# Sixteen copies out of PSUM move from VectorE to ScalarE in the attention, S5 and convolution parts of a decoder layer

## The chip, the cores and the metric

The kernel runs on one core of one Trainium2 chip. The metric is the device time of one execution in microseconds (us); the figure for a kernel is the median of several runs. PE is the matrix engine (TensorE), DVE is VectorE, ACT is ScalarE, POOL is GpSimd, and SP is the engine that issues most of the transfers.

## The reference

One layer of a hybrid decoder trunk with 512 tokens and a model width of 1024, all in float32. What is computed is a token mixer with three causal branches on the same normalised input, then a gated feed-forward part:

```python
h = rms_norm(x, pre1_w[l]) * (1.0 + sc1) + sh1
z = h @ w_in                       # one projection feeds all three branches
gq, gk, gv, ga, gr, mq, mk, mv, mi, mf, mo, su, zg = _split(z, IN_SIZES)
g_log = log_sigmoid(ga @ gla_a2 + gla_a_b) / GLA_GATE_NORM
o_gla = gla_attention(gq, gk, gv, g_log)           # chunked linear attention with decay
qk = silu(causal_dwconv(concat([mq, mk]), ml_conv_w, ml_conv_b))   # four taps
h_ml = mlstm_memory(qk_q, qk_k, mv, mi + ml_i_b, mf + ml_f_b)
y_s5 = gelu(s5_ssm(su, ...)); y_s5 = y_s5 * sigmoid(y_s5 @ s5_glu_w + s5_glu_b)
merged = gates0 * (y_gla @ proj_gla) + gates1 * (y_ml @ proj_ml) + gates2 * (y_s5 @ proj_s5)
x = x + (1.0 + gt1) * rms_norm(merged @ w_out, post1_w[l])
... swiglu feed-forward in the same sandwich of norms
```

The chunked gated attention needs the queries `gq`, the keys `gk` and the cumulated decay `cum`; the S5 branch needs its input `su`, and for each of four blocks of groups an impulse response, a matrix of transitions and a matrix of states.

## The kernel before

**Products.** Every float32 product is made of three matmuls of split operands: `passes` writes hi*hi, hi*lo and lo*hi into one bank of PSUM (lines 422 to 424, and 454 to 456 where the tokens are the stationary side). A weight arrives by a transfer as `raw`; ACT writes its upper part `hi`, and DVE the difference `lo`, L220, `lo<-raw,hi`. A product with `lo` therefore waits for a transfer, for ACT and for DVE. A bank of PSUM (`mm_bank` for the big products, `ax_bank` for auxiliary ones) is free again when its last reader is done.

**Stages.** The head (to about 66 us) normalises x and runs the "sweep": one pass over the input channels that fills six banks at once, `sweep_ps[0:2]` with gq, `[2:4]` with gk, `[4]` with the small gate inputs (ga, ii, lf), `[5]` with the first part of su. Then comes the gated attention (to about 190 us): the copies qT and kT, the decay (`log_sig`, whose first step is `t<-ax,pv` on ACT, L935 being its small product on PE), seven levels of pairwise scores (L1106, L1111), the running states `Sg` from kdT and gv (L1153, L1177), the normed output `og`, and its transposes (L1200). The S5 branch follows (to about 296 us) in five steps: `states(step-1)`, `params(step)`, `outputs(step-1)`. `states` makes PE's state product (L1283), then on DVE the rotated x5 and y5, a scan `v`, and the shifted `Xs`. `params` makes on DVE CA and `wp` out of four outer products o0 to o3, then a small `bs`, on PE the impulse responses (L1254), on some engine the copy `ks` of them, and a transfer of ks to memory and back as the matrix M. The mLSTM branch with the convolutions, the output projection and the feed-forward part come last.

**Order.** Between these steps the code calls `fill(n)`, which takes the next jobs from a list: gate products (`z` jobs, `ev_gate`), branch projections (`p` jobs, `merged`), the remaining inputs (`ev_gv`, `ev_gr`, `ev_su`, `ev_conv`) and, through DVE's `gacc`, the modulation rows. The order written so is not the order run: outside the regions fixed by hand, the framework's scheduler places the instructions of each engine by its own estimate of when they are ready. So an instruction that moves to another engine shifts others that the diff doesn't name. What is in the same order before and after: everything up to about 66 us, and everything behind about 344 us.

**Helpers.** `cp` (L232) is a copy on DVE, `ts` (L223), `tt` (L220) and `stt` (L226) are its operations with one scalar, two tensors, and both; `af` (L229) is an activation on ACT. As all calls go through them, the profile names these lines, and an instruction is told by its tiles (`kdT<-ax`). `st3` holds small statistics; `rstd` turns the sums of squares (ACT's `junk<-og`) into the norm's factors.

Of the kernel before, what the change touches and what calls it, by code (L numbers as in the profile page):

```python
# [8 lines left out]
AF = mybir.ActivationFunctionType  # L9
OP = mybir.AluOpType  # L10
# [166 lines left out]
def _body(tc, A, out):  # L177
    nc = tc.nc
    act, dve, pool, pe, sp = nc.scalar, nc.vector, nc.gpsimd, nc.tensor, nc.sync
    from contextlib import ExitStack  # L180
    with ExitStack() as ctx:
        _emit(tc, nc, ctx, ExitStack, A, out, act, dve, pool, pe, sp)


def _emit(tc, nc, ctx, ExitStack, A, out, act, dve, pool, pe, sp):
# [23 lines left out]
    def slot(name="s", dt=F32, tag="s"):  # L209
        return pools[tag].tile([128, 512], dt, tag=tag, name=name)  # L210
# [4 lines left out]
    def ax_bank(name="ax"):  # L215
        return axp.tile([128, 512], F32, tag="ax", name=name)


    def tt(e, o, a, b, op):
        e.tensor_tensor(out=o, in0=a, in1=b, op=op)  # L220

    def ts(e, o, a, s1, s2, op0, op1=OP.bypass):
        e.tensor_scalar(out=o, in0=a, scalar1=s1, scalar2=s2, op0=op0, op1=op1)  # L223

    def stt(o, a, s, b, op0, op1):
        dve.scalar_tensor_tensor(out=o, in0=a, scalar=s, in1=b, op0=op0, op1=op1)  # L226

    def af(o, i, f, **kw):
        act.activation(out=o, in_=i, func=f, **kw)  # L229

    def cp(o, i, e=dve):
        e.tensor_copy(out=o, in_=i)  # L232
# [12 lines left out]
    def P(name, i=None, n=1, rows=slice(0, 128)):  # L245
        o, w = _PV[name]
        return pv[rows, o:o + w] if i is None else pv[rows, o + i:o + i + n]

    def C(name, rows=slice(0, 128)):
        o, w = _CS[name]  # L250
        return cs[rows, o:o + w]
# [240 lines left out]
    for j, (c0, w) in enumerate(STRIPS):  # L492
        n = 512 // w
# [66 lines left out]
    w, h, u, r = (st[:, 4 * i:4 * i + 4] for i in range(4))  # L560
# [49 lines left out]
    sweep_ps = []  # L610
# [41 lines left out]
    def ev_conv(f):  # L652
        def e(ps):
            u = slot("conv", tag="v")
            w = lambda j: P("conv_w", f * 4 + j)
            ts(dve, u, ps, w(3), P("conv_b", f), OP.mult, OP.add)
            for j in range(3):
                d = 3 - j
                stt(u[:, d:512], ps[:, 0:512 - d], w(j), u[:, d:512], OP.mult, OP.add)
            af(u, u, AF.Silu)  # L660
            conv[f] = u
        return e
# [3 lines left out]
    def ev_su(f):  # L666
        def e(ps):
            u = slot("su")
            cp(u.rearrange("p (a n) -> p a n", a=8)[:, ::-1], ps.rearrange("p (n a) -> p a n", a=8))
            sp.dma_start(out=su_d[f].rearrange("a p n -> p a n"), in_=u.rearrange("p (a n) -> p a n", a=8))  # L670
            U[f] = upool.tile([128, 512], F32, tag="U", name="U")
            sp.dma_start(out=U[f], in_=su_d[f].rearrange("a (c g) n -> (a c) (g n)", g=8))
        return e
# [241 lines left out]
    qT, kT = {}, {}  # L915
    for p in range(2):
        qT[p], kT[p] = slot("gq"), slot("gk")
        af(qT[p], sweep_ps[p], AF.Copy, scale=0.125)
        cp(kT[p], sweep_ps[2 + p])
    ts(dve, ii[0:4], ii[0:4], P("i_b", rows=slice(0, 4)), None, OP.add)  # L920
    fill(1)
    cum = {}
# [10 lines left out]
    for p in range(2):  # L933
        ps = ax_bank()
# [149 lines left out]
    qk, qE, ecum, kdT, Sg = {}, {}, {}, {}, {}  # L1084
# [30 lines left out]
    n = 0  # L1115
# [15 lines left out]
    for p in range(2):  # L1131
        cv = cum[p].rearrange("p (t i) -> p t i", t=4)
        kd = slot("kd")
        kdv = kd.rearrange("p (t i) -> p t i", t=4)
        tt(dve, kdv[:, 0:3], cv[:, 0:3, 127:128].broadcast_to([128, 3, 128]), cv[:, 0:3], OP.subtract)
        af(kd[:, 0:384], kd[:, 0:384], AF.Exp, scale=1.0 / 16)
        tt(dve, kd[:, 0:384], kd[:, 0:384], kT[p][:, 0:384], OP.mult)
        ecum[p] = slot("ecum", tag="y")
        af(ecum[p], cum[p], AF.Exp, scale=1.0 / 16)
        qE[p] = slot("qE", tag="y")  # L1140
        tt(dve, qE[p], ecum[p], qT[p], OP.mult)
        ps = ax_bank()
        for t in range(3):
            pe.transpose(out=ps[:, t * 128:(t + 1) * 128], in_=kd[:, t * 128:(t + 1) * 128], identity=ident)
        kdT[p] = slot("kdT", tag="y")
        cp(kdT[p][:, 0:384], ps[:, 0:384])
    FL.until("gv")
    fill(2)
    for p in range(2):
        Sg[p] = slot("Sg", tag="y")  # L1150
        for t in range(3):
            ps = ax_bank()
# [13 lines left out]
    for t in range(4):  # L1166
        ps = [ax_bank(), ax_bank()]

        for h in range(4 if t else 0):
            p, hh = h // 2, h % 2  # L1170
# [3 lines left out]
        for h in range(4):  # L1174
            p, hh = h // 2, h % 2
            a = (t % 2) * 2 + hh
# [36 lines left out]
    def big(name):  # L1213
        return b4p.tile([128, 1024], F32, tag="b4", name=name)
# [3 lines left out]
    def outer(dst, a_r, a_i, k0, pr, sign):  # L1218

        pb = lambda x: x[:, pr, k0:k0 + 8].unsqueeze(3).broadcast_to([128, 4, 8, 16])  # L1220
        ab = lambda x: x[:, pr].unsqueeze(2).broadcast_to([128, 4, 8, 16])
        x = [slot(f"o{i}") for i in range(4)]
        w = lambda y: y.rearrange("p (a k c) -> p a k c", a=4, k=8)
        for i, (m, n) in enumerate(((P0, a_r), (P1, a_i), (P0, a_i), (P1, a_r))):
            tt(dve, w(x[i]), pb(m), ab(n), OP.mult)
        f = lambda y, r: y[r].rearrange("p (a n) -> p a n", a=4)
        d = dst.rearrange("p (a g n) -> p a g n", g=2, n=128)
        for g, r, q in ((0, even, odd), (1, odd, even)):
            tt(dve, d[r, :, g], f(x[0], r), f(x[1], r), OP.subtract)
            if sign > 0:  # L1230
                tt(dve, d[q, :, g], f(x[2], r), f(x[3], r), OP.add)
            else:
                stt(d[q, :, g], f(x[2], r), -1.0, f(x[3], r), OP.mult, OP.subtract)
# [3 lines left out]
    def params(b):  # L1237
        pr = slice(4 * b, 4 * b + 4)
        CA[b] = big("CA")
        outer(CA[b], s5c[:, 0], s5c[:, 1], 0, pr, -1)  # L1240
        wp = big("wp")
        outer(wp, bb[:, 0], bb[:, 1], 1, pr, 1)
        bs = slot("bs")
        bv = bs[:, 0:256].rearrange("p (g c) -> p g c", c=32)
        pool.memset(bs[:, 0:256], 0.0)
        b2 = bv[:, :, 0:16].rearrange("p (a g) c -> p a g c", g=2)
        for g, r, q in ((0, even, odd), (1, odd, even)):
            cp(b2[r, :, g], bb[r, 0, pr])
            cp(b2[q, :, g], bb[r, 1, pr])
        fill(1)  # L1250
        kp = ax_bank()
        for g in range(8):
            q = (g % 4) * 32
            mm(kp[q:q + 32, (g // 4) * 128:(g // 4 + 1) * 128], lhsT=bv[:, g], rhs=CA[b][:, g * 128:(g + 1) * 128],  # L1254
               start=True, stop=True, tile_position=(0, q))
        ks = slot("ks")
        cp(ks[:, 0:256], kp[:, 0:256])
        for j in range(2):
            stt(ks[:, j * 128:j * 128 + 16], C("dmask"), P("s5_d", 2 * b + j), ks[:, j * 128:j * 128 + 16],
                OP.mult, OP.add)  # L1260
        for q in range(4):
            sp.dma_start(out=kd_d.rearrange("(j q) c x -> q c j x", q=4)[q, :, 2 * b:2 * b + 2, 128:256],
                          in_=ks[q * 32:q * 32 + 16, 0:256].rearrange("p (j x) -> p j x", j=2))
        WT[b] = big("WT")
        for h in range(2):
            ps = ax_bank()
            for g in range(4):
                o = (h * 4 + g) * 128
                pe.transpose(out=ps[:, g * 128:(g + 1) * 128], in_=wp[:, o:o + 128], identity=ident)
            (lambda o, i: af(o, i, AF.Copy))(WT[b][:, h * 512:(h + 1) * 512], ps)  # L1270
        Mt[b] = big("M")
        for a in range(8):
            sp.dma_start(out=Mt[b][a * 16:(a + 1) * 16].rearrange("p (g x) -> p g x", g=8),
                         in_=kd_d[8 * b:8 * b + 8, :, 16 + 16 * a:144 + 16 * a].rearrange("g c x -> c g x"))
        fill(2)
# [49 lines left out]
    for step in range(5):  # L1325
        if step >= 1:
            states(step - 1)
        if step < 4:
            params(step)
        if step >= 1:  # L1330
            outputs(step - 1)
# [59 lines left out]
    ps = ax_bank()  # L1391
# [7 lines left out]
    for p in range(2):  # L1399
        ps = ax_bank()  # L1400
# [15 lines left out]
    for p in range(2):  # L1416
        qw[p] = mslot("qw")
        stt(qw[p], conv[p], 0.125, wI[p], OP.mult, OP.mult)
        ps = ax_bank()
# [8 lines left out]
    for p in range(2):  # L1428
        mem[p] = mslot("mem")
        for t in range(3):  # L1430
            ps = ax_bank()
# [277 lines left out]
    n = 22  # L1709
    for k in range(n - HOLD):  # L1710
        w = S.get(ffo_i[k], 4)
# [34 lines left out]
```

## Time and profile before

| | |
|---|---|
| median of three runs | 912.28 us (910.48 to 912.75) |
| the profiled execution | 910.4 us, of which 908.6 us are the span and 1.8 us lie around it |
| PE busy | 888.7 us, 98% of the span |
| DVE busy | 575.7 us, 63% |
| ACT busy | 331.0 us, 36% |
| mean granted TensorE clock | 0.989 |

PE is busy nearly all the time; the busy time of an engine includes matmuls that overlap, so 98% doesn't mean that PE does its work at its peak rate. The shares of the other engines are averages over stages that differ much. The timeline's start is the start of the span; "idle before" is the time that the engine stood before the row, and the arrow names what released it.

### The profile page before, as it was taken

The numbers are of one execution on the slowest core, as the hardware profiler recorded it, in microseconds if no ns is written. First come the engines' busy times: TensorE is split into PE (matmuls) and PEld (weight loads), VectorE is DVE, ScalarE is ACT, GpSimd is POOL, SyncE is SP. The second block draws the span as 40 slices with busy tenths as digits, with TensorE's granted clock in tenths as the row PEclk, the third lists the DMA queues.
The fourth block names the chain that finished last, engine by engine and source line by source line (L and its number), as shares of the span: only waits on it lengthen the run. The fifth ranks groups of instructions, "written<-read, shape, count | busy, mean of one in ns | idle before, by whom it ended". The sixth has DMA issues, their size and how long they took to land.

```text
span 908.6 us, 11582 instructions
## 1 busy us (share of the span) xinstructions
PE 888.7 (98%) x4334; PEld 723.1 (80%) x4334; DVE 575.7 (63%) x1144; ACT 331.0 (36%) x512; POOL 24.9 (3%) x68
## 2 busy tenths in 40 slices
PE   9999999999989999999999989999999999999997
PEld 7667887878878878788888868888888888888885
DVE  6748999979879884966679497544433333322215
ACT  4339323431442462722334444333222332211113
POOL 2010000000000000010000000000000000000000
PEclk7999999999999999999999999999999999999999
DMA  9661341233443442345456533533333323322303
GB/s 364 251 193 47 116 128 58 82 125 111 154 139 108 121 116 93 131 127 172 153 175 226 199 140 117 185 116 117 118 126 130 113 93 116 115 93 97 113 1 139
DMA packets 52193, 120.79 MB, mean 133 GB/s; under 512 B 13797, under 2 KB 19429, under 8 KB 52137
## 3 DMA queue, kind: packets, MB, share of 16 engines
q1 hardware_dynamic: 49944, 115.92, 38.0%
q0 software_dynamic: 1040, 2.38, 1.1%
q10 hardware_dynamic: 1152, 1.75, 0.5%
q8 instruction: 34, 0.56, 0.3%
q14 instruction: 23, 0.18, 0.1%
HBM read 113.21 MB, written 6.82 MB: 132 GB/s over the span
## 4 chain that ended last, share of the span: by engine, by line
PE 77%; DVE 17%; issue 2%; ACT 2%; DMA 1%; SPq 0%; DVEq 0%; ACTq 0%
PE mm L422 16%; PE mm L423 16%; PE mm L424 16%; PE y L1527 5%; PE y L1526 5%; PE y L1528 5%; DVE lo L220 3%; PE mm L455 2%; PE mm L454 2%; PE mm L456 2%; DVE ST L1111 1%; DVE Qp L220 1%; DVE o L220 1%; DVE D L220 1%; PE ax L1318 1%
## 5 line engine op out<-in xcount | busy, mean ns | idle before, releaser
L229 ACT ACTIVATE hi<-raw 128x1024 fp32r<-128x1024 f32 (+2 forms) x157 | 151.9, 971 | 382.2 <-PE mm L423 156.2
L220 DVE TENSOR_TENSOR lo<-raw,hi 128x1024 fp32r<-128x1024 f32 (+2 forms) x157 | 174.6, 1114 | 155.6 <-ACT hi L229 155.0
L424 PE MATMUL mm<-h2hi,lo 128*128 128x512 f32 x320 | 124.6, 389 | 0.0
L423 PE MATMUL mm<-h2lo,hi 128*128 128x512 f32 x320 | 124.6, 389 | 0.0
L422 PE MATMUL mm<-h2hi,hi 128*128 128x512 f32 x320 | 124.5, 389 | 0.0
L424 PE MATMUL mm<-hT,lo 128*128 128x512 f32 x280 | 110.7, 395 | 3.1 <-DVE lo L220 3.1
L422 PE MATMUL mm<-hT,hi 128*128 128x512 f32 x280 | 112.3, 401 | 0.2 <-ACT hT L229 0.2
L423 PE MATMUL mm<-hT,hi 128*128 128x512 f32 x280 | 111.0, 396 | 0.4 <-DVE hT L226 0.4
L422 PEld LDWEIGHTS mm<-h2hi,hi 128*128 128x128 f32 x320 | 60.1, 188 | 12.5
L424 PEld LDWEIGHTS mm<-h2hi,lo 128*128 128x128 f32 x320 | 60.1, 188 | 12.4
L423 PEld LDWEIGHTS mm<-h2lo,hi 128*128 128x128 f32 x320 | 60.1, 188 | 12.3
L1528 PE MATMUL y<-hi,g 128*128 128x512 f32 x176 | 68.5, 389 | 0.0
L1527 PE MATMUL y<-lo,g 128*128 128x512 f32 x176 | 68.5, 389 | 0.0
L1526 PE MATMUL y<-hi,g 128*128 128x512 f32 x176 | 68.3, 389 | 0.0
L220 DVE TENSOR_TENSOR sg<-sg,mm 128x512 f32<-128x512 f32 x36 | 24.7, 685 | 64.8 <-PE mm L424 64.7
L422 PEld LDWEIGHTS mm<-hT,hi 128*128 128x128 f32 x280 | 53.2, 190 | 15.7 <-issue 4.0
L424 PEld LDWEIGHTS mm<-hT,lo 128*128 128x128 f32 x280 | 53.2, 190 | 14.6 <-DVE lo L220 3.5
L423 PEld LDWEIGHTS mm<-hT,hi 128*128 128x128 f32 x280 | 53.1, 190 | 11.9 <-DVE hT L226 1.2
L226 DVE SCALAR_TENSOR_TENSOR gacc<-raw,cact,gacc 128x512 f32<-128x512 f32 x56 | 41.9, 748 | 21.9 <-DMA raw<-ada 21.3
L455 PE MATMUL mm<-lo,hT 128*128 128x512 f32 x128 | 50.5, 394 | 0.4 <-DVE lo L220 0.4
L454 PE MATMUL mm<-hi,hT 128*128 128x512 f32 x128 | 49.8, 399 | 0.0
L456 PE MATMUL mm<-hi,hT 128*128 128x512 f32 x128 | 49.7, 391 | 0.0
(311 smaller groups left out, 1393.9 us busy)
## 6 DMA issues: line engine op xcount, KB each, us to landing
raw<-ada SPq DMA_DIRECT2D x48, 512.0 KB, 3.5
raw<-ffn SPq DMA_DIRECT2D x44, 512.0 KB, 3.3
raw<-wzg SPq DMA_DIRECT2D x24, 512.0 KB, 3.2
raw<-ffo SPq DMA_DIRECT2D x22, 512.0 KB, 3.3
raw<-wpr SPq DMA_DIRECT2D x24, 256.0 KB, 2.7
raw<-wout SPq DMA_DIRECT2D x8, 512.0 KB, 4.3
raw<-sweep SPq DMA_DIRECT2D x8, 384.0 KB, 8.5
xT<-xT SPq DMA_DIRECT2D x4, 512.0 KB, 5.6
```

The source lines that it names most:

```text
L220: e.tensor_tensor(out=o, in0=a, in1=b, op=op)
L226: dve.scalar_tensor_tensor(out=o, in0=a, scalar=s, in1=b, op0=op0, op1=op1)
L229: act.activation(out=o, in_=i, func=f, **kw)
L422: mm(ps, lhsT=whi, rhs=xhi, start=first, stop=False)
L423: mm(ps, lhsT=whi, rhs=xlo, start=False, stop=False)
L424: mm(ps, lhsT=wlo, rhs=xhi, start=False, stop=last)
L454: mm(ps[t], lhsT=xh[:, tk], rhs=hi[:, sl], start=(k == 0), stop=False)
L455: mm(ps[t], lhsT=xh[:, tk], rhs=lo[:, sl], start=False, stop=False)
L456: mm(ps[t], lhsT=xl[:, tk], rhs=hi[:, sl], start=False, stop=(k == 7))
L1526: mm(ps, lhsT=xhi, rhs=whi[:, sl], start=first, stop=False)
L1527: mm(ps, lhsT=xhi, rhs=wlo[:, sl], start=False, stop=False)
L1528: mm(ps, lhsT=xlo, rhs=whi[:, sl], start=False, stop=last)
```

## The change

Sixteen instructions that read a bank of PSUM become activations on ACT instead of operations on DVE: the first of the four taps of each convolution (`ev_conv`, 4 of them), the copy of the S5 input (`ev_su`, 4; it is written in reverse order with a stride), the keys (`kT`, 2), the transposed decayed keys (`kdT`, 2, 128x384) and the impulse responses (`ks`, 4, 128x256).

```diff
@@ -653,7 +653,7 @@
         def e(ps):
             u = slot("conv", tag="v")
             w = lambda j: P("conv_w", f * 4 + j)
-            ts(dve, u, ps, w(3), P("conv_b", f), OP.mult, OP.add)
+            af(u, ps, AF.Identity, scale=w(3), bias=P("conv_b", f))
             for j in range(3):
                 d = 3 - j
                 stt(u[:, d:512], ps[:, 0:512 - d], w(j), u[:, d:512], OP.mult, OP.add)
@@ -666,7 +666,7 @@
     def ev_su(f):
         def e(ps):
             u = slot("su")
-            cp(u.rearrange("p (a n) -> p a n", a=8)[:, ::-1], ps.rearrange("p (n a) -> p a n", a=8))
+            af(u.rearrange("p (a n) -> p a n", a=8)[:, ::-1], ps.rearrange("p (n a) -> p a n", a=8), AF.Copy)
             sp.dma_start(out=su_d[f].rearrange("a p n -> p a n"), in_=u.rearrange("p (a n) -> p a n", a=8))
             U[f] = upool.tile([128, 512], F32, tag="U", name="U")
             sp.dma_start(out=U[f], in_=su_d[f].rearrange("a (c g) n -> (a c) (g n)", g=8))
@@ -916,7 +916,7 @@
     for p in range(2):
         qT[p], kT[p] = slot("gq"), slot("gk")
         af(qT[p], sweep_ps[p], AF.Copy, scale=0.125)
-        cp(kT[p], sweep_ps[2 + p])
+        af(kT[p], sweep_ps[2 + p], AF.Copy)
     ts(dve, ii[0:4], ii[0:4], P("i_b", rows=slice(0, 4)), None, OP.add)
     fill(1)
     cum = {}
@@ -1143,7 +1143,7 @@
         for t in range(3):
             pe.transpose(out=ps[:, t * 128:(t + 1) * 128], in_=kd[:, t * 128:(t + 1) * 128], identity=ident)
         kdT[p] = slot("kdT", tag="y")
-        cp(kdT[p][:, 0:384], ps[:, 0:384])
+        af(kdT[p][:, 0:384], ps[:, 0:384], AF.Copy)
     FL.until("gv")
     fill(2)
     for p in range(2):
@@ -1254,7 +1254,7 @@
             mm(kp[q:q + 32, (g // 4) * 128:(g // 4 + 1) * 128], lhsT=bv[:, g], rhs=CA[b][:, g * 128:(g + 1) * 128],
                start=True, stop=True, tile_position=(0, q))
         ks = slot("ks")
-        cp(ks[:, 0:256], kp[:, 0:256])
+        af(ks[:, 0:256], kp[:, 0:256], AF.Copy)
         for j in range(2):
             stt(ks[:, j * 128:j * 128 + 16], C("dmask"), P("s5_d", 2 * b + j), ks[:, j * 128:j * 128 + 16],
                 OP.mult, OP.add)
```

The scheduler places the instructions anew from 66 to 344 us. Three places of the new order matter for what follows.

The first is ACT at the end of the sweep; `t<-ax,pv` is the first step of the decay. Before:

```order
L881 DMA s5c<-s5c 128x512
L229 ACTIVATE hi<-raw 128x1024 x3
L229 ACTIVATE gq<-mm 128x512 x2
L229 ACTIVATE t<-ax,pv 128x512
L229 ACT_TABLE_LOAD
```

After:

```order
L881 DMA s5c<-s5c 128x512
L229 ACTIVATE hi<-raw 128x1024 x3
L229 ACTIVATE su<-ax 128x8x64
L229 ACTIVATE gq<-mm 128x512
L229 ACTIVATE gk<-mm 128x512
L229 ACTIVATE gq<-mm 128x512
L229 ACTIVATE gk<-mm 128x512
L229 ACTIVATE t<-ax,pv 128x512
L229 ACT_TABLE_LOAD
```

The copy su now stands ahead of the two gq, and a copy gk behind each of them, so `t` comes behind five copies where it came behind two.

The second is DVE in `states(0)` and `params(1)`; lo_2252 is the split of a gate's weights. Before, from the first x5 that reads the scan:

```order
L220 TENSOR_TENSOR x5_2045<-v_2051,ph_645 128x512
L220 TENSOR_TENSOR y5_2046<-v_2051,ph_645 128x512
L220 TENSOR_TENSOR o1_2113<-pw_734,bb_733 128x512
L220 TENSOR_TENSOR o2_2114<-pw_734,bb_733 128x512
L220 TENSOR_TENSOR lo_2191<-raw_2057,hi_2190 128x512
L220 TENSOR_TENSOR CA_2098<-o0_2099,o1_2100 64x4x128 x2
L226 SCALAR_TENSOR_TENSOR CA_2098<-o2_2101,o3_2102 64x4x128 x2
L220 TENSOR_TENSOR merged_2149<-sg_1762,mm_2136 128x512
L220 TENSOR_TENSOR lo_2252<-raw_2134,hi_2251 128x1024
L220 TENSOR_TENSOR Xs_2092<-x5_2045,y5_2046 64x4x63 x4
L220 TENSOR_TENSOR o3_2115<-pw_734,bb_733 128x512
L220 TENSOR_TENSOR wp_2111<-o0_2112,o1_2113 64x4x128 x2
```

After, the same piece:

```order
L226 SCALAR_TENSOR_TENSOR gacc_1797<-raw_2061,cact_91,gacc_1797 128x512
L220 TENSOR_TENSOR CA_2098<-o0_2099,o1_2100 64x4x128 x2
L220 TENSOR_TENSOR lo_2191<-raw_2057,hi_2190 128x512
L226 SCALAR_TENSOR_TENSOR CA_2098<-o2_2101,o3_2102 64x4x128 x2
L220 TENSOR_TENSOR merged_2149<-sg_1762,mm_2136 128x512
L220 TENSOR_TENSOR Xs_2092<-x5_2045,y5_2046 64x4x63 x4
L220 TENSOR_TENSOR o3_2115<-pw_734,bb_733 128x512
L220 TENSOR_TENSOR wp_2111<-o0_2112,o1_2113 64x4x128 x2
L226 SCALAR_TENSOR_TENSOR gacc_1797<-raw_2061,cact_91,gacc_1797 128x512
L220 TENSOR_TENSOR lo_2252<-raw_2134,hi_2251 128x1024
L232 COPY bs_2124<-bb_733 64x4x16 x4
L220 TENSOR_TENSOR lo_2273<-raw_2194,hi_2272 128x512
```

lo_2252 has moved behind the four Xs, o3 and the first two wp, one gacc has moved in front of it, and lo_2191 stands between the CA.

The third is DVE in `states(1)` and `params(2)`; lo_2565 is again the split of a gate's weights. Before:

```order
L220 TENSOR_TENSOR merged_2505<-sg_2017,mm_2492 128x512
L226 SCALAR_TENSOR_TENSOR CA_2401<-o2_2404,o3_2405 64x4x128 x2
L226 SCALAR_TENSOR_TENSOR gacc_2278<-raw_2378,cact_91,gacc_2278 128x512
L220 TENSOR_TENSOR Xs_2395<-x5_2356,y5_2357 64x4x63 x4
L220 TENSOR_TENSOR o3_2418<-pw_734,bb_733 128x512
L220 TENSOR_TENSOR wp_2414<-o0_2415,o1_2416 64x4x128 x2
L220 TENSOR_TENSOR lo_2565<-raw_2490,hi_2564 128x1024
L232 COPY bs_2427<-bb_733 64x4x16 x4
```

After:

```order
L226 SCALAR_TENSOR_TENSOR CA_2401<-o2_2404,o3_2405 64x4x128 x2
L220 TENSOR_TENSOR merged_2505<-sg_2017,mm_2492 128x512
L220 TENSOR_TENSOR Xs_2395<-x5_2356,y5_2357 64x4x63 x4
L220 TENSOR_TENSOR o3_2418<-pw_734,bb_733 128x512
L220 TENSOR_TENSOR wp_2414<-o0_2415,o1_2416 64x4x128 x2
L226 SCALAR_TENSOR_TENSOR gacc_2278<-raw_2378,cact_91,gacc_2278 128x512
L232 COPY bs_2427<-bb_733 64x4x16 x4
L220 TENSOR_TENSOR lo_2565<-raw_2490,hi_2564 128x1024
```

The four bs now stand ahead of lo_2565. Further up, the split lo_2371 moved from ahead of `states(1)`'s x5_2356 to behind it. On PE, between the products of L1283 that x5_2356 reads and the first one that needs lo_2565, stand 82 products of 512 columns before and 89 after, and the eight of L1254 besides.

## Rows read from the trace of the kernel before

**Rows 1.** Page, busy time, share and instructions of each engine.
```profile
PE 888.7 (98%) x4334; PEld 723.1 (80%) x4334; DVE 575.7 (63%) x1144; ACT 331.0 (36%) x512; POOL 24.9 (3%) x68
```

**Rows 2.** Stretches: length, busy of each engine, PEclk, DMA share, GB/s.
```profile
66.00:148.00 82.00, 81.29 (x418) 67.31 (x416) 78.15 (x212) 40.78 (x54) 0.00 (x0) 1.00 0.30 93
...
186.00:189.40 3.40, 3.40 (x14) 2.31 (x14) 3.40 (x14) 0.39 (x1) 0.00 (x0) 0.51 0.00 0
...
260.00:336.00 76.00, 75.98 (x473) 63.49 (x472) 67.95 (x108) 38.18 (x52) 2.70 (x10) 1.00 0.41 126
```

**Rows 3.** Timeline of PE, 86 to 93.5 us: start, duration, instruction, idle before.
```profile
87.53 0.50 PE L455 MATMUL mm<-lo,hT 128*128 128x512 f32 x1 [0.38 <-DVE lo L220]
```

**Rows 4.** Timeline of PE, 146.9 to 150 us.
```profile
149.24 0.68 PE L1177 MATMUL ax<-gv,ST 128*128 128x128 f32 x4 [1.05 <-DVE Sg L226]
```

**Rows 5.** Timeline of PE, 178 to 192 us.
```profile
185.35 4.32 PE L1200 MATMUL ax<-ident,og 128*128 128x128 f32 x16 [1.64 <-DVE og L226]
```

**Rows 6.** Timeline of PE, 244 to 262 us.
```profile
255.62 0.50 PE L424 MATMUL mm<-hT,lo 128*128 128x512 f32 x1 [3.08 <-DVE lo L220]
```

**Rows 7.** DVE by line and form: busy us, mean ns, idle before.
```profile
L232 DVE COPY su<-mm 128x512 f32<-128x512 f32 x3 | 2.1, 685 | 0.0
...
L232 DVE COPY ks<-ax 128x256 f32<-128x256 f32 x4 | 1.7, 419 | 0.2 <-PE ax L1254 0.2
...
L232 DVE COPY kdT<-ax 128x384 f32<-128x384 f32 x2 | 1.1, 550 | 0.0
...
L223 DVE TENSOR_SCALAR conv<-mm,pv 128x512 f32<-128x512 f32 x4 | 3.2, 807 | 0.1
```

**Rows 8.** ACT by line and form.
```profile
L229 ACT ACTIVATE sg<-mm,pv 128x512 f32<-128x512 f32 x24 | 16.2, 675 | 1.9 <-PE mm L424 1.8
...
L229 ACT ACTIVATE hT<-h,s1c 128x512 fp32r<-128x512 f32 x8 | 5.6, 724 | 14.4 <-DVE h L226 14.4
...
L229 ACT ACTIVATE gq<-mm 128x512 f32<-128x512 f32 x2 | 1.2, 598 | 3.1 <-PE mm L424 3.0
...
L229 ACT ACTIVATE s<-ax 128x256 f32<-128x256 f32 x4 | 1.5, 380 | 0.0
```

**Rows 9.** Timeline of ACT, 62 to 73 us.
```profile
67.99 0.69 ACT L229 ACTIVATE t<-ax,pv 128x512 f32<-128x512 f32 x1 [3.46 <-PE ax L935]
```

**Rows 10.** Timeline of PE, 63 to 69 us.
```profile
66.31 0.40 PE L424 MATMUL ax<-hT,lo 128*128 128x512 f32 x1
```

**Rows 11.** Timeline of ACT, 148 to 203 us.
```profile
189.01 2.07 ACT L229 ACTIVATE yhi<-ax 128x512 fp32r<-128x512 f32 x4 [4.28 <-PE ax L1200]
```

**Rows 12.** Timeline of DVE, 66 to 97 us.
```profile
72.60 0.69 DVE L220 TENSOR_TENSOR g<-g,t 128x512 f32<-128x512 f32 x1 [1.49 <-ACT t L229]
...
86.27 1.21 DVE L220 TENSOR_TENSOR lo<-raw,hi 128x1024 fp32r<-128x1024 f32 x1
```

**Rows 13.** Timeline of DVE, 150 to 190 us.
```profile
166.86 0.46 DVE L223 TENSOR_SCALAR st<-st 128x16 f32<-128x16 f32 x3 [1.00 <-ACT junk L229]
...
184.95 4.28 DVE L226 SCALAR_TENSOR_TENSOR og<-og,st,gr 128x128 f32<-128x128 f32 x16
```

**Rows 14.** Timeline of DVE, 203 to 226 us.
```profile
218.28 1.22 DVE L220 TENSOR_TENSOR lo<-raw,hi 128x1024 fp32r<-128x1024 f32 x1
...
219.41 1.70 DVE L220 TENSOR_TENSOR Xs<-x,y 64x252 f32<-64x252 f32 x4
...
223.16 0.82 DVE L232 COPY bs<-bb 64x64 f32<-64x64 f32 x4
```

**Rows 15.** Timeline of PE, 219.5 to 222 us.
```profile
220.67 0.39 PE L423 MATMUL mm<-ylo,hi 128*128 128x512 f32 x1
220.89 0.39 PE L424 MATMUL mm<-hT,lo 128*128 128x512 f32 x1
```

**Rows 16.** Timeline of DVE, 230 to 262 us.
```profile
254.34 1.23 DVE L220 TENSOR_TENSOR lo<-raw,hi 128x1024 fp32r<-128x1024 f32 x1
```

**Rows 17.** Timeline of PE, 225.5 to 227 us.
```profile
225.97 0.64 PE L1254 MATMUL ax<-CA,bs 128*32 128x128 f32 x16
```

## Prediction

> **What bounds the kernel now.** I read the page's busy times first: PE works in 888.7 of the 908.6 us of the span [rows 1]. So the change can only gain where PE waits, and it loses wherever it makes PE wait anew; an instruction that becomes cheaper on VectorE (DVE) is worth nothing by itself. Next the table of stretches [rows 2]. The sixteen moved instructions all lie between 66 and 344 us. In 66 to 148 us PE is busy for 81.29 of 82.00 us, and DVE for 78.15: two engines at their limit side by side. In 260 to 336 us PE is busy for 75.98 of 76.00, so the convolutions, the mo bank and two of the four impulse responses lie under a full PE. Then PE's timeline row by row, for the rows that carry an idle time. Between 66 and 344 us there are only four worth a name: 0.38 us at 87.53 [rows 3], 1.05 at 149.24 [rows 4], 1.64 at 185.35 [rows 5] and 3.08 at 255.62 [rows 6], each released by DVE. The reader is to see that DVE is late four times in 280 us, 6.15 us in all, and that the last is half of it.
>
> **What is taken off DVE.** By the rows of the forms [rows 7]: four su copies at 0.685 us, two kT copies of the same size, two kdT at 0.550, four ks at 0.419, four first taps at 0.807: 2.74 + 1.37 + 1.10 + 1.68 + 3.23 = 10.1 us.
>
> **What is put on ScalarE (ACT).** It has room: 40.78 us busy in 66 to 148 us, 38.18 of 76 in 260 to 336 [rows 2]. Its reads of a 128x512 bank of PSUM cost 0.598 us (gq, which stands beside kT), of 128x256 0.380 [rows 8]. kdT (128x384) lies between the two. The first tap takes a scale and a bias from a column each; with a bias column the row is 0.675 (sg), and the highest 128x512 row here is 0.724 (hT, a bias column too) [rows 8]. So the tap costs 0.675 at least, and, as two columns are in no row, I bound it above by DVE's 0.807; the four lie under the full PE, and without that cover the worst case is 4 x 0.807 = 3.2 us. The sum for ACT is about 9 us, most of it free. What counts is what queues behind a moved copy.
>
> Here a rule speaks against the change. The gq row is 0.087 us shorter than the su row on DVE [rows 7, 8]. The Trainium skill, page "ScalarE: Activation LUTs", section "Rules for kernel authors", tells authors to do simple arithmetic on VectorE and not on ScalarE. For float32 out of PSUM the rows here say otherwise. By the rows the six full-width copies cost less than before; by the rule they would cost more, and a mechanism of that kind is rival B.
>
> **Step 1, the start of the attention: later.** Before, ACT copies the two gq banks, then waits 3.46 us for the small product of L935, and takes t<-ax,pv at 67.99 [rows 9]. After, the order puts su, gq, gk, gq, gk ahead of that t. su waits for the last product of the sweep, which starts at 66.31 and lasts 0.40 [rows 10], so for 66.71. Four copies out of PSUM in a row take 2.07 us on ACT, 0.52 each [rows 11]; five take 2.6, and t starts at 69.3 and not at 67.99: **+1.3**. If only starts count, (2.07 - 0.60) / 3 = 0.49 each, it is +1.2; if each took 0.72 without overlap, 66.71 + 3.6 = 70.3 and +2.3. DVE can't hide it: it waits for that t (1.49 us at 72.60 [rows 12]), so the time it saves there only lengthens its wait. It then runs without pause to the lo at 86.27 [rows 12] for which PE waits at 87.53 [rows 3]. PE is dense before and behind, so it ends 1.3 late.
>
> **Step 2, Sg at 149.24: earlier.** On DVE's way there are three su and two kdT fewer. That is 3 x 0.685 + 2 x 0.550 = 3.2 us [rows 7], of which 1.3 pays for DVE's own later start. The other 1.9 can take away the wait of 1.05. But the kdT copies now stand on ACT ahead of a split of weights. Bounds 0 and -1.05; I take **-0.8**, nearer the far end.
>
> **Step 3, og at 185.35: nothing.** DVE starts the norm's statistics at 166.86 after a wait of 1.00 us for ACT's squares [rows 13], which hang on products of PE. Time saved earlier on DVE ends in this wait, and the chain on to the sixteen og at 184.95 (4.28 us) [rows 13] keeps its distance to PE. Bounds: 0, and a gain of 1.64 + 1.7 if DVE does come earlier, since PE's clock from 186.0 to 189.4 us is at 0.51, its 1.2 GHz level [rows 2], and such a stretch at full clock would need half of its 3.4 us.
>
> **Step 4, states(0): a new wait.** The change moves an instruction that it does not touch. lo<-raw,hi (lo_2252) starts at 218.28 and the four Xs behind it at 219.41; bs follows at 223.16 [rows 14]. After, the Xs, the o and the two wp stand ahead of that lo: 223.16 - 219.41 = 3.75 us. The two gacc change place inside the piece and cancel. So lo starts at 218.28 + 3.75 = 222.03 and ends 1.22 later, at 223.25. PE takes its first product with it at 220.89 [rows 15] without a wait. So PE waits **+2.4**. Bounds 2.2 and 2.6: one product of 0.22 (220.67 to 220.89 [rows 15]) more or less ahead. It would be nothing if DVE came to this piece 2.4 us earlier against PE; but it begins with the x that reads PE's own states product, so both start together.
>
> **Step 5, states(1) at 255.62: less of an old wait.** On DVE one more 128x512 split (lo_2371) and the four bs come ahead of the lo that starts at 254.34 [rows 16]: about 0.69 + 0.82 = 1.5 us. On PE seven more products of 512 columns and the eight of L1254 come between the states product and the one that waits: 7 x 0.22 + 0.64 [rows 17] = 2.2, where matmuls overlap at their ends by a tenth. The wait of 3.08 [rows 6] falls by **0.6** (bounds 0.3 and 0.7).
>
> **Elsewhere: nothing.** Chains 2 and 3, conv and ks lie in the stretch with 0.02 us of idle PE. ks is read by DVE next and then by a transfer that has steps to land; if that cover were gone, 4 x 0.42 = 1.7 us. Behind 344 us no order changes.
>
> **Sum.** 1.3 - 0.8 + 0 + 2.4 - 0.6 = +2.3 us. The profiled execution took 910.4, so 912.7 for one like it; on the median of the three runs, 912.28, it gives **914.6**. A measurement of this kernel can't tell 0.3%, 2.7 us, from no change: the three runs themselves span 2.3 us. The forecast is thus at the upper edge of "no change".
>
> **Rivals.**
> B, slower still: ACT is the slower copier, with 0.72 a copy. Then t starts at 70.3 (+2.3), the later kdT keeps the wait at 149.24 as it is (no -0.8), and the sum is 2.3 + 2.4 - 0.6 = +4.1 (916.4). It decides from 0.6 us a copy. For it: five copies in a row stand between PE and the decay, and su is written reversed with a stride, in no ACT row before. Against it: 0.598 for gq [rows 8].
> C, faster: DVE is the true limit from 66 to 190 us, and what is taken from it comes back. The waits of 1.05 and 1.64 and the half-speed 1.7 go, 1.3 is lost at the start, and steps 4 and 5 give +1.8: -1.3; if states(0) is not late either, -3.7 (908.6). For it: 78.15 of 82.00 busy. Against: the 1.00 at 166.86, where DVE itself waits. It decides if that wait is not refilled. The Trainium skill, page "Perfetto Trace Analysis", section "Optimizing Scalar/DVE Operations", says that with DVE saturated it may make sense to offload to Scalar; no row before shows which wait that would end.
> D, nothing moves: the later start is swallowed at 149.24 and the order at states(0) finds slack. +0.2 to +1, or 913. For it: behind 260 us DVE has 8 of 76 us to spare [rows 2]. Against: the 3.75 us stand in the order.
>
> **How the numbers follow.** Forecast 47% (own range +1 to +3.5: 913.3 to 915.8; a third of it beyond +2.7), B 18%, C 20%, D 15%. Slower by over 0.3%: 17 of the 47 and 17 of B's 18, together 34%. Faster: 14 of C's 20, its form of -3.7, 14%. The rest, 52%, within. The range goes from 909.5 (most of C outside) to 918 (1.6 above B's sum): 47 + 15 + 14 + 7 = 83%.
>
> **What would show it.** In the trace after: t<-ax,pv on ACT at about 69.3; the idle at 149 below 0.5; a PE row L424 mm<-hT,lo near 224 us that waits some 2.4 us for DVE's lo; the wait at 255.62 (a few us later) at 2.4 to 2.8. The prediction is wrong if no row near 224 waits, if og at 185 waits for less than 1 us, or if the copies on ACT take over 0.65 us.

## The result and the profile after

The changed kernel takes 917.11 us in the median of five runs (914.94 to 917.6); the kernel before 912.28 (five runs, 909.29 to 912.75). The medians lie 4.8 us apart. The ratio estimated from all runs is 1.0062 with a 95% interval of 1.0043 to 1.0082: slower by 0.62%, some 5.7 us, where 914.6 was forecast. The 40 executions of the kernel before that were taken beside the experiments lie in two bands, 17 from 909.4 to 910.7 us and 23 from 911.3 to 912.7, and its first profile (910.4) is from the lower one. The profiled execution took 917.49 us with a span of 915.7.

First the moved copies themselves, in the forms of ACT (busy us, mean ns, idle before), in the kernel after:

```profile
L229 ACT ACTIVATE conv<-mm,pv 128x512 f32<-128x512 f32 x4 | 3.0, 762 | 0.0
...
L229 ACT ACTIVATE su<-mm 128x512 f32<-128x512 f32 x3 | 1.7, 579 | 0.0
L229 ACT ACTIVATE ks<-ax 128x256 f32<-128x256 f32 x4 | 1.5, 382 | 8.6 <-PE ax L1254 8.6
...
L229 ACT ACTIVATE gk<-mm 128x512 f32<-128x512 f32 x2 | 1.2, 616 | 0.0
...
L229 ACT ACTIVATE kdT<-ax 128x384 f32<-128x384 f32 x2 | 1.0, 489 | 1.0 <-PE ax L1144 1.0
```

Against [rows 7] each copy is shorter on ACT than it was on DVE: su 579 for 685 ns, kdT 489 for 550, ks 382 for 419, and the first tap, with two columns, 762 for 807. The Trainium skill, page "ScalarE: Activation LUTs", section "Rules for kernel authors", sends simple arithmetic (add, mul) to VectorE, with a speed in bf16 as its ground; for float32 out of PSUM these rows show the opposite, and the rows decide. So the loss is not in what the copies themselves take.

ACT's timeline behind the sweep, after (start, duration, instruction):

```profile
66.73 0.60 ACT L229 ACTIVATE su<-ax 128x512 f32<-128x512 f32 x1 [6.51 <-PE ax L424]
...
68.65 0.63 ACT L229 ACTIVATE gk<-mm 128x512 f32<-128x512 f32 x1
69.13 0.72 ACT L229 ACTIVATE t<-ax,pv 128x512 f32<-128x512 f32 x1
```

The decay's first step starts at 69.13 and not at 67.99 [rows 9]. Here too the order counts and not only the number of copies. Before, ACT made the two gq while PE was still at work on the last bank of the sweep:

```profile
63.24 1.30 ACT L229 ACTIVATE gq<-mm 128x512 f32<-128x512 f32 x2 [2.97 <-PE mm L424]
```

After, they stand behind su, which can't start before 66.7, and ACT is idle for 6.51 us ahead of it. DVE and PE behind it, after:

```profile
69.89 0.75 DVE L223 TENSOR_SCALAR g<-ax,pv 128x512 f32<-128x512 f32 x1 [1.36 <-ACT t L229]
73.78 0.69 DVE L220 TENSOR_TENSOR g<-g,t 128x512 f32<-128x512 f32 x1 [3.14 <-ACT t L229]
...
87.44 1.21 DVE L220 TENSOR_TENSOR lo<-raw,hi 128x1024 fp32r<-128x1024 f32 x1
```

```profile
88.70 0.50 PE L455 MATMUL mm<-lo,hT 128*128 128x512 f32 x1 [1.12 <-DVE lo L220]
```

DVE, which has three copies fewer to make here, waits 1.36 and 3.14 us where it waited 1.49 [rows 12]. The lo that PE needs starts 1.17 us later than before, and PE waits 1.12 for 0.38 [rows 3].

At the running states Sg, PE and DVE after:

```profile
148.87 0.67 PE L1153 MATMUL ax<-gv,kdT 128*128 128x256 f32 x2 [0.63 <-DVE Sg L226]
150.43 0.68 PE L1177 MATMUL ax<-gv,ST 128*128 128x128 f32 x4 [0.90 <-DVE Sg L226]
```

```profile
147.99 0.72 DVE L226 SCALAR_TENSOR_TENSOR Sg<-Sg,ecum,ax 64x128 f32<-64x128 f32 x2
...
149.56 0.73 DVE L226 SCALAR_TENSOR_TENSOR Sg<-Sg,ecum,ax 64x128 f32<-64x128 f32 x2
...
166.55 1.12 DVE L226 SCALAR_TENSOR_TENSOR og<-gv,st,ax 128x128 f32<-128x128 f32 x4 [2.49 <-PE ax L1177]
168.53 0.46 DVE L223 TENSOR_SCALAR st<-st 128x16 f32<-128x16 f32 x3 [0.86 <-ACT junk L229]
```

In the place of one wait of 1.05 us [rows 4] there are two, 0.63 and 0.90. The same two pairs of Sg on DVE, before:

```profile
146.64 0.73 DVE L226 SCALAR_TENSOR_TENSOR Sg<-Sg,ecum,ax 64x128 f32<-64x128 f32 x2
...
148.37 0.73 DVE L226 SCALAR_TENSOR_TENSOR Sg<-Sg,ecum,ax 64x128 f32<-64x128 f32 x2
```

DVE comes to them 1.35 and 1.19 us later than before, although eight copies fewer stand on its way (four su, two kT, two kdT). Rows of the S5 parameters stand between the pairs in both kernels. What is new is how many stand ahead of the first pair: nine more than before (x, y, ph and w, 2.9 us by their durations). The scheduler has filled the time of the three su and two kdT (3.2 us [rows 7]) with them. Further on DVE waits 2.49 us at 166.55 for PE's last products of L1177, which start 2.0 us later than before (165.51 for 163.49), and then 0.86 for ACT's squares.

PE and DVE at states(0), after:

```profile
223.06 0.39 PE L423 MATMUL mm<-ylo,hi 128*128 128x512 f32 x1
226.13 0.50 PE L424 MATMUL mm<-hT,lo 128*128 128x512 f32 x1 [2.69 <-DVE lo L220]
...
227.24 0.63 PE L422 MATMUL mm<-hT,hi 128*128 128x512 f32 x1
...
230.58 0.39 PE L424 MATMUL mm<-hT,lo 128*128 128x512 f32 x1
```

```profile
220.45 1.70 DVE L220 TENSOR_TENSOR Xs<-x,y 64x252 f32<-64x252 f32 x4
...
224.19 0.75 DVE L226 SCALAR_TENSOR_TENSOR gacc<-raw,cact,gacc 128x512 f32<-128x512 f32 x1
224.86 1.22 DVE L220 TENSOR_TENSOR lo<-raw,hi 128x1024 fp32r<-128x1024 f32 x1
```

The reader sees the forecast wait: 2.69 us at 226.13, released by the lo that starts at 224.86, behind Xs, o, wp and a gacc. Also to be seen is what was not forecast: behind the wait a product lasts 0.63 us and not 0.39 until 230. The stretches around it, after (length, busy of each engine, PEclk, DMA share, GB/s):

```profile
222.00:226.00 4.00, 1.45 (x7) 0.87 (x5) 3.92 (x7) 0.00 (x0) 1.03 (x2) 1.00 0.03 9
226.00:230.50 4.50, 4.37 (x12) 3.46 (x13) 3.50 (x9) 0.00 (x0) 0.00 (x0) 0.62 0.87 281
```

PEclk is 0.62 over 226.0 to 230.5 us; by the durations of single rows it fell to half of 2.4 GHz for some 3.4 us, from less than 1 us behind the 2.7 us in which PE stood still. At og and at states(1), after:

```profile
187.03 4.41 PE L1200 MATMUL ax<-ident,og 128*128 128x128 f32 x16 [1.29 <-DVE og L226]
...
191.93 0.63 PE L422 MATMUL mm<-hT,hi 128*128 128x512 f32 x1
```

```profile
251.63 0.50 PE L424 MATMUL mm<-hT,lo 128*128 128x512 f32 x1 [0.27 <-DVE lo L220]
...
261.20 0.97 PE L1254 MATMUL ax<-CA,bs 128*32 128x128 f32 x16 [1.11 <-DVE bs L232]
262.79 0.50 PE L424 MATMUL mm<-hT,lo 128*128 128x512 f32 x1 [0.62 <-DVE lo L220]
```

The wait for og is 1.29 us for 1.64 [rows 5], and the products right behind the transposes run at half clock too. At states(1) three waits of 0.27, 1.11 and 0.62 us stand for the one of 3.08 [rows 6].

### The profile page after: what moved, and what is told of

The parts are those of the page before. It is cut to its first block, busy times and chain, and to the rows that moved or that the text cites. A ratio compares the mean times of both kernels' runs of the same rounds, so it can differ in the third digit from the quotient of the medians.

```text
span 915.7 us, 11586 instructions
## 1 busy us (share of the span) xinstructions
PE 892.8 (97%) x4334; PEld 725.0 (79%) x4334; DVE 568.2 (62%) x1128; ACT 336.8 (37%) x526; POOL 24.9 (3%) x68
## 4 chain that ended last, share of the span: by engine, by line
PE 69%; DVE 12%; DMA 3%; issue 2%; ACT 1%; DVEq 0%; ACTq 0%
PE mm L424 14%; PE mm L422 14%; PE mm L423 14%; PE y L1526 5%; PE y L1527 5%; PE y L1528 5%; DVE lo L220 2%; PE mm L456 2%; PE mm L455 2%; DMA raw<-ada 2%; PE mm L454 2%; DVE o L220 1%; DVE gacc L226 1%; PE ax L1319 1%; PE ax L1318 1%
## 5 line engine op out<-in xcount | busy, mean ns | idle before, releaser
L454 PE MATMUL mm<-hi,hT 128*128 128x512 f32 x128 | 50.6, 401 | 0.0
```

What stands on the lines that cost most here:

```text
L454: mm(ps[t], lhsT=xh[:, tk], rhs=hi[:, sl], start=(k == 0), stop=False)
```

## Where the time went: the stages by PE's own rows

PE's rows before and behind the moved region are the same in all kernels, so the distances between starts can be compared: from the small product of L935 to the first L1153 (the scores), on to the first product behind the transposes of L1200 (Sg and og), on to the first L1421 (S5 and what is filled in beside it). The head is left out, since L935 starts at 65.5 to 66.9 us in these profiles; in the first profile of before and in that of after it starts at the same time to 0.01 us. The last column is what the half-clock products of that last stage cost: for each 512-column row that lasts about 0.63 us, the distance to the next start beyond 0.23, and for a first one behind a wait or behind the transposes, which lasts about 0.79, beyond the 0.34 of such a row at full clock. All in us, from the profiled execution of each kernel:

| kernel | scores | Sg and og | S5 | of it half clock |
|---|---|---|---|---|
| before | 72.9 | 49.9 | 141.0 | 0 |
| before, second profile | 72.9 | 49.9 | 143.2 | 2.2 |
| after | 73.6 | 50.9 | 145.5 | 2.0 |
| ks alone | 72.9 | 49.9 | 145.5 | 2.0 |
| all but ks | 73.7 | 50.7 | 143.9 | 2.0 |
| start alone | 73.7 | 50.6 | 143.5 | 2.6 |
| all but the start | 72.9 | 49.0 | 144.8 | 1.4 |
| middle alone | 72.9 | 49.1 | 145.0 | 2.6 |
| middle and fill | 72.9 | 49.1 | 140.2 | 0 |
| fill alone | 72.9 | 50.0 | 140.2 | 0.8 |

After less before: +0.7 in the scores, +1.0 at Sg and og, +2.5 in S5 without the half clock, +2.0 of half clock. The spans lie 7.1 us apart; the rest is +0.6 at a wait for weights near 490 us, which the second profile of before shows too (0.60 us at 488.73 there), and 0.3 behind it. The half clock too is in the second profile of before (experiment 8). So 2.6 of the 7.1 us are of a kind that an execution of before has too, and 4.2 go with the change; the interval of the ratio is 3.9 to 7.5 us.

## The experiments

Order theory: the change loses because the scheduler, with other engines for sixteen instructions, places other instructions later, above all the lo at states(0). Rival, the copy theory: the loss is in the copies, in what they take on ACT or delay there.

**1. Only ks** on ACT. The order outside S5 stays as before.

```diff
-        cp(ks[:, 0:256], kp[:, 0:256])
+        af(ks[:, 0:256], kp[:, 0:256], AF.Copy)
```

> Only the four ks copies go to ACT; the attention keeps the order of before on every engine, and on DVE the piece at states(0) has the new order (lo behind Xs, o, wp). Order theory (the loss is a split of weights that comes late at states(0)): PE waits 2.5 to 2.8 us there near 221 to 224 us, its clock falls to half for some 3.4 us behind that wait (1.6 us), the wait of states(1) shrinks by about 0.5; together +3.7 us, 916.0. Copy theory (the loss is what the moved copies themselves take or delay on ACT at the start of the attention): nothing there is touched, so 912.3 within 1 us.

Measured: 914.31 us against 911.51 for before on the same chip, ratio 1.0046 (1.0029 to 1.0062). That is 2.8 us by the medians and 4.2 by the ratio, where +3.7 was expected of the one theory and nothing of the other. PE's rows with a wait in the S5 part of this kernel:

```profile
223.27 0.50 PE L424 MATMUL mm<-hT,lo 128*128 128x512 f32 x1 [2.69 <-DVE lo L220]
...
248.78 0.50 PE L424 MATMUL mm<-hT,lo 128*128 128x512 f32 x1 [0.27 <-DVE lo L220]
...
258.35 0.97 PE L1254 MATMUL ax<-CA,bs 128*32 128x128 f32 x16 [1.12 <-DVE bs L232]
259.94 0.50 PE L424 MATMUL mm<-hT,lo 128*128 128x512 f32 x1 [0.62 <-DVE lo L220]
```

They are the waits of the changed kernel, to 0.01 us: 2.69, 0.27, 1.12, 0.62. Four copies of 0.4 us, each cheaper than before, cost S5 2.5 us, without the half clock, by the place of instructions that they don't touch. A kernel with ks on ACT and that split held in its old place was not tried; experiments 6 and 7 try the like at states(1).

**2. All but ks**: the change, with that line back on DVE.

> The change without its ks part: the order at states(0) and states(1) is that of before, all else as in the change. Order theory: the 2.7 us wait and the half-speed stretch near 224 us are gone, the wait of 3.1 us at states(1) is back: 917.1 - 3.7 = 913.4. Copy theory: twelve of the sixteen copies still stand on ACT, so 916 to 917.

Measured: 914.9 us, ratio 1.0041 (1.0027 to 1.0055). The wait at states(0) is gone and that at states(1) is back, but 913.4 was expected. The table shows why it is more: 2.0 of half clock in its profile, mostly behind the wait of states(1), where I had booked none, and a wait of 0.44 us near 310 for a transfer of the S5 outputs. What the start and the middle cost, +0.7 and +0.8 in the first two columns, is still there.

**3. The start alone**: the two kT and the first su.

```diff
-        cp(kT[p], sweep_ps[2 + p])
+        af(kT[p], sweep_ps[2 + p], AF.Copy)
...
-            cp(u.rearrange("p (a n) -> p a n", a=8)[:, ::-1], ps.rearrange("p (n a) -> p a n", a=8))
+            (cp if f else (lambda o, i: af(o, i, AF.Copy)))(u.rearrange("p (a n) -> p a n", a=8)[:, ::-1], ps.rearrange("p (n a) -> p a n", a=8))
```

> Only the two kT and the first su copy go to ACT; the order at the states is that of before. Start theory: the first step of the decay (t on ACT) starts at 69.1 and not at 68.0, PE's wait near 88 us grows from 0.4 to 1.1, PE is 0.7 us late at 132 us, and it stays so: 913.0 to 913.5. Rival: the later start is swallowed at the wait of 1.05 us at 149: 912.3.

Measured: 914.35 us in the median of twelve runs (909.49 to 915.71), ratio 1.0025 (1.0012 to 1.0039), more than the 913.0 to 913.5 expected. The later start is not swallowed at 149: +0.7 in the scores, another +0.6 at Sg and og. Together that is 1.3 us, a little more than the delay of t, which is 1.14 in the change (69.13 less 67.99). The S5 part is as before but for 2.6 of half clock.

**4. All but the start**: the change with kT and the first su on DVE.

> The change with the two kT and the first su copy back on DVE. If the start costs its 0.7 us and no more: 916.4. If the two waits of 0.63 and 0.90 us near 149 us, in the place of one of 1.05, come from the later start too: 915.5 or less. If they come from the new order of DVE (S5 parameters between the Sg rows), they stay.

Measured: 913.2 us, ratio 1.0016 (1.0003 to 1.0030). More comes back than the 0.7: Sg and og take 49.0 us, 0.9 less than before and 1.9 less than in the change. PE's waits there:

```profile
148.02 0.67 PE L1153 MATMUL ax<-gv,kdT 128*128 128x256 f32 x2 [0.38 <-DVE Sg L226]
...
151.07 0.60 PE L1177 MATMUL ax<-gv,ST 128*128 128x128 f32 x4
...
184.69 4.26 PE L1200 MATMUL ax<-ident,og 128*128 128x128 f32 x16 [0.91 <-DVE og L226]
```

0.38 and 0.91 stand where before had 1.05 and 1.64 [rows 4, 5]. So with these copies off DVE the attention gains, if it has not been started late. But DVE is not earlier at Sg. Its second pair of Sg in this kernel:

```profile
149.23 0.73 DVE L226 SCALAR_TENSOR_TENSOR Sg<-Sg,ecum,ax 64x128 f32<-64x128 f32 x2
```

Counted from the start of L935 it is 0.8 us later than before. What is new is PE's order: eleven products of 512 columns stand between the last L1153 and the first L1177, where none stood before, and cover that pair. PE's last products of L1177 and DVE's start of og then come 0.9 and 0.8 us earlier than before, counted so. How much of the 0.9 us is DVE's freed time and how much PE's order was not tried apart. The S5 part keeps the wait of states(0).

**5. The middle alone**: su 1 to 3, kdT and the first taps.

> Only su 1 to 3, kdT and the first taps go to ACT; the start of the attention and the states keep the order of before. Relief theory (DVE freed between 90 and 150 us does come back if the start is not late): between the first Sg product and the end of the og transposes 0.9 us are gained as in the kernel without the start's copies, and the rest is as before: 910.6 where before is at 911.5. Copy theory (each moved copy costs on ACT): 912 to 913.

Measured: 910.77 us in the median of eleven runs (ten from 909.12 to 913.07, and one of 2051.61 that the ratio leaves out) against 911.33, ratio 0.9994 (0.9984 to 1.0003). Sg and og gain the same 0.9 us, with the same eleven products between. S5 takes 1.4 more than before without the half clock, of which 0.91 is a wait for a transfer of the S5 outputs near 309. The interval holds no change too, so the gain is shown by the rows of one stage and not by the total time.

**6. The middle, and one job moved.** In `states`, one filling job goes from behind the scan to ahead of the rotation, in each of its four calls; nothing else is touched.

```diff
@@ states @@
-        fill(2)
+        fill(3)
...
-        fill(2)
+        fill(1)
```

> As the kernel with su 1 to 3, kdT and the first taps on ACT, and one filling job of states() moved from behind the scan to ahead of it. By the order of rows the lo that PE awaits for 3.1 us at states(1) then comes in time. Order theory: 3 us and whatever half-speed stretch follows that wait are gained: 907 to 908. Rival: the wait only moves to another row: 910.6.

Measured: 907.95 us (906.82 to 908.87), ratio 0.9959 (0.9945 to 0.9972). It beats both kernels. PE's only wait from 222 to 270 us, and the lo that it waits for, in this kernel:

```profile
252.20 0.50 PE L424 MATMUL mm<-hT,lo 128*128 128x512 f32 x1 [0.53 <-DVE lo L220]
```

```profile
250.92 1.23 DVE L220 TENSOR_TENSOR lo<-raw,hi 128x1024 fp32r<-128x1024 f32 x1
...
252.73 1.70 DVE L220 TENSOR_TENSOR Xs<-x,y 64x252 f32<-64x252 f32 x4
```

The lo now stands ahead of the four Xs, as in states(0) of the kernel before; 3.08 us have become 0.53. Some of it came back as waits of 0.68, 0.22 and 0.34 us for wp and M near 290 and 305 us, so that S5 takes 140.2 us for 141.0. This profile has no half-speed stretch, neither here nor at og. By the table the two stages gain 1.6 us against the first profile of before and 3.8 against the second, which has such stretches. Whether other executions of this kernel are free of them was not seen.

**7. That job moved, no copy.**

> The kernel before with that one filling job moved, no copy on ACT. Order theory: the wait of 3.1 us is worth the same without the moved copies: 908 to 909. If it needs the freed DVE, 911 to 912.

Measured: 909.12 us, ratio 0.9979 (0.9968 to 0.9989), a little less gain than expected. The reordering is worth 2 us by itself. The middle copies bring 1.2 more by the medians of experiments 6 and 7, whose intervals just overlap, and the 0.9 at Sg and og by the rows.

**8. The kernel before, a second profile.**

> The kernel before, unchanged, a second profile. Its runs lie between 909.4 and 912.7. Clock theory (whether a half-speed stretch follows a wait of 3 us is a matter of the single execution): the rows are the same to 0.1 us, and a stretch at half clock stands behind the wait near 255 us in one profile and not in another, or at another place. Rival: the clock falls at the same places each time.

Measured: 912.43 us. The rows at states(1):

```profile
252.04 0.39 PE L423 MATMUL mm<-ylo,hi 128*128 128x512 f32 x1
255.50 0.80 PE L424 MATMUL mm<-hT,lo 128*128 128x512 f32 x1 [3.07 <-DVE lo L220]
...
256.95 0.63 PE L424 MATMUL mm<-hT,lo 128*128 128x512 f32 x1
...
259.21 0.39 PE L424 MATMUL mm<-hT,lo 128*128 128x512 f32 x1
```

The stretch 254 to 258 us in this profile, and then in the first profile of before:

```profile
254.00:258.00 4.00, 2.50 (x6) 2.02 (x7) 3.88 (x9) 0.00 (x0) 0.00 (x0) 0.68 0.36 128
258.00:262.00 4.00, 4.00 (x31) 2.99 (x29) 3.03 (x5) 1.06 (x1) 0.00 (x0) 0.90 0.72 262
```

```profile
254.00:258.00 4.00, 2.38 (x10) 1.98 (x11) 3.88 (x9) 0.00 (x0) 0.00 (x0) 1.00 0.29 100
258.00:262.00 4.00, 4.00 (x38) 3.13 (x37) 3.15 (x5) 0.14 (x1) 0.00 (x0) 1.00 0.82 285
```

The same program, the same wait (3.07 and 3.08 us), but here the clock is 0.68 and there 1.00. The half clock behind it differs from execution to execution; with og's it costs 2.2 us in one and none in the other, out of the 3 us by which the runs of this kernel spread.

## Why the prediction was right, and where it was not

The sign and the range held; the single number was 2.5 us low. The range of 909.5 to 918 held by its width, which is luck as far as the steps go: they came to 4.2 us by the rows, where their sum was 2.3, and the forecast's own range, 913.3 to 915.8, did not hold. And the chances put 52% on a change within 0.3% and 34% on a slower kernel; the less likely of the two came.

**Step 1, right.** t starts at 69.13 (69.3 forecast). The 1.3 us come in two parts, 0.7 before the scores end and 0.6 at Sg and og (experiment 3). One reading in it is wrong without harm: DVE does not run without pause from 72.60 to the lo, but waits 1.20 us at 77.06, for ACT's t again.

**Step 2, wrong.** "The other 1.9 can take away the wait of 1.05", taken at -0.8. Beside the late start it came to +0.4: Sg and og take 1.0 more than before, of which 0.6 is the start's. The step took the 3.2 us of copies for time by which DVE comes earlier to Sg. It doesn't: the scheduler put 2.9 us of S5 parameter rows ahead of the first pair, and DVE came 1.35 us later. Without the start the same copies gain 0.9 (experiments 4 and 5), there too with DVE later at Sg, and with another order on PE. And I treated the two as terms that add, and they don't: the start costs 1.3 beside nothing and 2.4 beside the middle copies (72.9 + 49.1 against 73.7 + 50.7). What the rows show of it is that PE is the late one then: DVE waits 2.49 us for its product at 166.55, a wait that the kernel before didn't have. Why the scheduler orders PE and DVE so beside the late start was not tried apart.

**Step 3, right** in its mechanism: the statistics still wait for ACT's squares (0.86 for 1.00 [rows 13]), and og for the statistics (1.29 for 1.64 [rows 5]). From the start of the statistics to the start of og it is 18.1 us before and after. With the middle alone og's wait falls to 0.91, more than nothing.

**Step 4, right, and too small.** 2.69 us where 2.4 were forecast, with 2.6 as the bound. The two gacc do not cancel: lo starts 4.41 us behind the Xs and not 3.75, with a gacc of 0.75 us just ahead of it. By the distances of starts the wait costs PE 3.2 us: PE is 2.4 us later than before ahead of it and 7.0 behind the half-clock stretch, and 1.4 of the difference are the half clock's. Experiment 1 shows the wait without the other parts, experiment 2 the other parts without it.

**Step 5, right in the sum.** 2.00 us idle for 3.08; but each restart costs more, since L1254 takes 0.97 for 0.64 [rows 17], and by the distances of starts the gain is 0.6, as forecast. It was not foreseen that bs itself would be awaited, for 1.11.

**Left out: the clock.** I read the only profile of before as the rule: full clock behind the wait of states(1), half clock at og hidden by the wait for og. So the sum has no term for a half-speed stretch behind the new wait, where the profile of after shows one. Experiment 8 shows that before, too, can have it, behind its own wait; in experiments 1 and 4 it stands behind the new wait, in 2, 3 and 5 behind the old one. By these profiles the change moves the stretch more than it adds it. How often each kernel has it was not measured. The two profiles of before hint at it: the one without a costly stretch took 910.4 us and the one with it 912.43, and they belong to the two bands of its runs, the lower at a mean granted clock of 0.989 to 0.993 and the upper at 0.987 to 0.990. Whether what lies between 4.2 us by the rows and 4.8 by the medians or 5.7 by the ratio is that or chance stays open.

**Rivals.** B got the size (+4.1) for a wrong reason: no copy on ACT is slow, and five in a row start 0.48 us apart. It was right that the -0.8 would not come, though not by a late kdT. C's gain is there without the late start (experiments 4 and 5), but it is 0.9 us, in part by PE's order, and beside the late start it gave nothing. D fell, since the 3.75 us of other rows did bind and the late start was not swallowed. On C the Trainium skill, page "Perfetto Trace Analysis", section "Optimizing Scalar/DVE Operations", says that offloading to Scalar may make sense with DVE saturated; that holds here for the middle copies, by 0.9 us in one stage and without a sure gain in the total, and not for the whole change. Of the experiments' two theories the copy theory fell for S5 with experiment 1. At the start it holds: there 1.3 us are lost by what copies delay on ACT (experiment 3).

## What to carry to other kernels

Where a scheduler places the instructions, moving one to another engine is an edit of the whole order: compare the orders, look for splits and copies that the full engine awaits and that came to stand behind others, and price those first. Beware of what comes to stand at the head of a chain on the engine that takes it: here that cost 1.3 us, and copies in the middle cost nothing that the total shows. Time taken off an engine is not time by which its next needed row comes earlier, as the scheduler may fill it with other rows. And terms that share a chain don't add: ask for each gain on an engine whether the other side is late by then.

## What was not expected of the hardware

The granted clock fell to half at the end of a wait of PE of 2.7 to 3.2 us, or within 1 us or so behind it, in seven profiles of eight that have such a wait: 7 products of 512 columns at half speed (1.4 us) in five of them, 13 (2.6 us) in two. In the eighth, the first profile of before, it stayed full behind 3.08 us. Behind the 0.53 us of experiments 6 and 7 it stayed full too. At the og transposes it fell in all seven profiles in which PE had waited 1.29 us or more for og, and in none of the three with about 0.9 (experiments 4 to 6). That costs little, since PE is paced by og there: 0.6 to 0.8 us, where it outlasts the transposes.
